# Gates of the last two branches ahead of the branches' own weights, in eight tiles; one attention over chosen keys among the heads

## The chip, the cores and the metric

The kernel runs on one core of a Trainium2 chip. Its engines are TensorE (PE; matmuls, and PEld for its weight loads), VectorE (DVE), ScalarE (ACT), GpSimd (POOL) and SyncE (SP), which issues the weight transfers. The metric is the device time of one execution in microseconds (us), the median of several runs. A difference is told in us or per cent of that time.

## The reference, cut to what matters

Two transformer blocks run one after the other over 256 tokens of width 1024. The first (a convolution, gated linear attention and a mixture of experts) is not touched. The second ends its mixing half with four branches, each gated by the block's normalised input u:

```python
u = rms_norm(h, norm_mix_pre[l])
z = u @ w_in[l]
(hq, hf, hi, hg, pz, sq, sk, sv, iq, ik, iw, mq) = jnp.split(z, split_pts, axis=-1)
y_a = hgrn2_mixer(hq, hf, hi, hg, lb_all[l], hgrn_norm[l])   # branch 0: a recurrence of 4 heads
y_b = pool_mixer(pz, pool_w[l], pool_scale[l])               # branch 1: means over windows
y_c = dsa_mixer(sq, sk, sv, iq, ik, iw)                      # branch 2: attention over chosen keys
...
y_m = mem_attention(mq, mk, mv)                              # branch 3: attention into a memory
for bi, y in enumerate((y_a, y_b, y_c, y_m)):
    term = jax.nn.sigmoid(u @ w_gate[l, bi]) * (y @ w_branch[l, bi])
    merged = term if merged is None else merged + term
h = h + rms_norm(merged @ w_out[l], norm_mix_post[l])
u = rms_norm(h, norm_ffn_pre[l])
gt, up = jnp.split(u @ w_ffn_gate_up[l], 2, axis=-1)
h = h + rms_norm((jax.nn.silu(gt) * up) @ w_ffn_down[l], norm_ffn_post[l])
```

A gate is a product of 256 × 1024 by 1024 × 1024; a branch's own product is 256 × 256 by 256 × 1024. All is in float32.

## The kernel before, in words

Each float32 operand of a large product is split into a rounded half and a remainder (hi and lo for weights, uh and ul or yh and yl for activations). A product is then three matmuls, in `Split.mm`: hi by hi (L186), hi by the activation's remainder (L187), the weights' remainder by hi (L188). The rounding of a weight piece of 128 × 2048 is one ScalarE instruction (L170); its remainder is split between VectorE (1280 columns, L172) and GpSimd (768 columns, L173). Pieces of 1 MB come by SyncE in a fixed order (`stream2`), and three buffers each for the incoming piece, for hi and for lo go round in turn. So the rounding of a piece waits until the piece three before it has been used by its last matmul.

In `second()` the order of calls is: `recall` (memory attention), `pooled`, `choose` for the two blocks of 128 tokens, `recur(0)` to `recur(3)` (the HGRN2 heads), `chosen(1)` and `chosen(0)` (attention over the chosen keys), then `branch(1)`, `branch(3)`, `branch(0)`, `branch(2)`, then w_out. A scheduler orders the instructions of each engine with this order as priority and with its own estimate of durations; it interleaves gate matmuls, which need only u, with the heads. Each engine then goes through its own list in order. From w_out on, the lists of ScalarE, VectorE and GpSimd are written out by hand (`tc.manual_schedule`), those of TensorE are not.

The last head, `recur(3)`, ends in a chain: decay products on TensorE (L1322) that VectorE copies under a mask (L1323), products with the values and the state (L1328, L1339, L1343), the square on ScalarE (L1349), the sum over the head (L1351), the root and its reciprocal (L1353, L1354), two multiplications (L1355, L1356) and the split into yh and yl (L178, L179). `chosen` has scores (L1444, L1451), a maximum (L1453), the exponential (L1382), sum and scaling (L1383, L1384), transposes (L1386) and the products with the values (L1398).

A branch of before computes, for each quarter of the 1024 columns (two blocks of 128), the gate's product in `dn.turned`, the branch's product with yh and yl, the sigmoid on ScalarE into one of two `sg` tiles, the product of both on VectorE (L1497), and the addition to `merged` on GpSimd (L1498). Its weights are taken ahead of its gate's two times two pieces. w_out takes `merged` split into four quarters mh and ml; `unit(t, half, kh)` is one product of 12 matmuls with 512 columns each. The normalisation and the split into uh and ul that the FFN needs follow.

Of the kernel before, what the change touches and what calls it, by code (L numbers as in the profile page):

```python
# [8 lines left out]
F32 = mybir.dt.float32  # L9
# [3 lines left out]
AF = mybir.ActivationFunctionType  # L13
OP = mybir.AluOpType
# [3 lines left out]
P = 128  # L18
T = 256
# [109 lines left out]
class Stream:  # L129
# [20 lines left out]
    def take(self):  # L150
        self.ahead(1)
        return self.ready.pop(0)
# [954 lines left out]
def second(tc, A, k, out):  # L1107
    nc = tc.nc
    V, S, G = nc.vector, nc.scalar, nc.gpsimd
    ident = k.cav("ident")  # L1110
    col2 = k.col2
    ones = k.cav("ones")
    k.n_a1, k.n_a2, k.n_sg = 6, 2, 2
    st_ = k.stream
    take = st_.take

    def pt(shape=(P, 512)):
        return k.ps.tile(list(shape), F32, tag="ps", name="pst", bufs=k.n_ps)

    def mx(shape=(P, 512)):  # L1120
        return k.ps.tile(list(shape), F32, tag="mx", name="mxt", bufs=8 - k.n_ps)

    with ExitStack() as es:
        ap = es.enter_context(tc.tile_pool(name="act2", bufs=1, side="right", reuse_waits="tile"))
        tp = es.enter_context(tc.tile_pool(name="tmp2", bufs=2, side="right", reuse_waits="tile"))
# [23 lines left out]
        sp = Split(nc, k.hi, k.lo)  # L1149
        dn = Dense(k, sp, take, pt)  # L1150
# [86 lines left out]
        for t in range(2):  # L1237
            p = mx((P, 4, P))
# [34 lines left out]
        yh, yl = {}, {}  # L1273
# [199 lines left out]

        merged = None

        def branch(b):

            nonlocal merged
            first = merged is None
            if first:  # L1480
                merged = ap.tile([P, NB, T], F32, tag="merged", name="merged")
            bh, bl = sp.weights(take(), 2)
            for half in range(2):
                def gate_in(i, o):
                    if i % 2 == 0:
                        return
                    blk = half * 4 + i - 1
                    p = pt((P, 2, T))
                    for j in range(2):
                        s = slice((blk + j) * P, (blk + j + 1) * P)  # L1490
                        sp.mm(p[:, j], lambda c: (bh[:, c, s], bl[:, c, s]), lambda c: (yh[b][:, c], yl[b][:, c]), 2)
                    sg = tp.tile([P, 2, T], F32, name="sg", bufs=k.n_sg)
                    S.activation(sg[:], dn.banks[i // 2][:], AF.Sigmoid)
                    if first:
                        V.tensor_tensor(merged[:, blk:blk + 2], sg[:], p[:], op=OP.mult)
                    else:
                        V.tensor_tensor(sg[:], sg[:], p[:], op=OP.mult)  # L1497
                        G.tensor_tensor(merged[:, blk:blk + 2], merged[:, blk:blk + 2], sg[:], op=OP.add)  # L1498

                dn.turned(X, gate_in)  # L1500

        recall(0)
        pooled()
# [2 lines left out]
        choose(0)  # L1506
        recur(0)
        recur(1)
        recur(2)
        recur(3)  # L1510
        chosen(1)
        chosen(0)
        branch(1)
        branch(3)
        post = ap.tile([P, 2, D], F32, tag="ln2", name="post")
        nc.sync.dma_start(post[:], A["rows2"][:, 2 * D:4 * D].rearrange("o (a d) -> o a d", a=2)
                            .to_broadcast([P, 2, D]))
        branch(0)
        branch(2)
        gain = ap.tile([P, D], F32, tag="gain", name="gain")  # L1520
        nc.sync.dma_start(gain[:], A["rows2"][:, 5 * D:].to_broadcast([P, D]))

# [19 lines left out]
        for q in range(4):  # L1542
            s = slice(2 * q, 2 * q + 2)
# [13 lines left out]
        with tc.manual_schedule(engines={E.Activation, E.DVE, E.Pool}):  # L1557
# [7 lines left out]
            a, b = [add_normed(t, banks[t], post[:, 0]) for t in range(2)]  # L1565
# [74 lines left out]
        a, b = [add_normed(t, banks[t], post[:, 1], True) for t in range(2)]  # L1640
        with tc.manual_schedule(engines={E.Activation, E.DVE, E.Pool}):
            go(a, a, a, b, a, b, b, b)
        for t in range(2):
            for half in range(2):
                s = slice(half * 512, half * 512 + 512)
# [3 lines left out]
def body(tc, A, out):  # L1649
# [6 lines left out]
    with ExitStack() as es:  # L1656
# [25 lines left out]
        with ExitStack() as mid:  # L1682
# [15 lines left out]
            experts(tc, A, k)  # L1698
        k.stream.open([A["s2"][i] for i in range(A["s2"].shape[0])])
        second(tc, A, k, out)  # L1700


# [31 lines left out]
def stream2(f):  # L1734

    w, gate, br = f["w_in_2"][0], f["w_gate_2"][0], f["w_branch_2"][0]
    gu, dn = f["w_ffn_gate_up_2"][0], f["w_ffn_down_2"][0]
    out = []

    def add(m):  # L1740
        out.extend(m.reshape(2, 4, P, 512).transpose(0, 2, 1, 3).reshape(2, P, PIECE))

    def rows(m):

        out.append(m.reshape(2, P, D).transpose(1, 0, 2).reshape(P, PIECE))

    add(np.concatenate([w[:, 1536:1792], w[:, 1024:1280]], axis=1))
    add(w[:, 512:1024])
    add(np.concatenate([w[:, 2760:3016], w[:, 2688:2752], w[:, 2048:2112], w[:, 2752:2760], w[:, 2112:2176],
                        np.zeros((D, 56), np.float32)], axis=1))  # L1750
    add(w[:, 2176:2688])
    add(w[:, 0:512])
    add(np.concatenate([w[:, 1792:2048], w[:, 1280:1536]], axis=1))
    for b in (1, 3, 0, 2):
        rows(br[b])
        for half in range(2):
            add(gate[b][:, half * 512:half * 512 + 512])
    for half in range(2):
        add(f["w_out_2"][0][:, half * 512:half * 512 + 512])
    for i in range(11):  # L1760
        add(np.concatenate([gu[:, 256 * i:256 * i + 256], gu[:, D_FF + 256 * i:D_FF + 256 * i + 256]], axis=1))
        if i:
            rows(dn[256 * i - 256:256 * i])
    rows(dn[2560:])
    m = f["w_mem_kv_2"][0].reshape(2, 4, P, 512).transpose(0, 2, 1, 3).reshape(2, P, PIECE)
    return np.stack(out), m
# [66 lines left out]
```

## Time and profile before

| | us |
|---|---|
| median of 3 runs (1702.92 to 1703.82) | 1702.96 |
| profiled execution, its own time | 1702.62 |
| its span | 1700.8 |
| TensorE busy in the span | 1491.7 (88%) |
| VectorE, ScalarE, GpSimd busy | 547.6, 468.5, 483.3 |

The granted clock of TensorE is 0.957 of full over the whole span. The span has three parts: the first block's dense half to about 310 us, its experts, bound by the transfer of their weights, to about 1190 us, and the second block. The change is in the second block, between 1240 and 1510 us. A line of the timeline gives start, duration, engine, source line, operation, what is written and read, tile and count, and in brackets the idle time of the engine ahead of it with the instruction that ended it.

### The profile page before, as it was taken

What the parts mean: (1) busy time and instruction counts of PE and PEld (TensorE: products, weight loads), DVE (VectorE), ACT (ScalarE), POOL (GpSimd) and SP (SyncE); (2) the same over time, 40 slices, a digit from 0 to 9 for tenths busy, and PEclk for the clock granted to TensorE, in tenths of its full rate; (3) what the DMA queues carried; (4) which work ended last, traced back from release to release, by engine and by line L of the source; (5) the groups of instructions that cost most, each with busy time, mean ns of one, the idle gap of its engine ahead of it and who ended that gap; (6) DMA issues with size and microseconds to landing.
All of it is one profiled execution on the core that took longest, in us unless ns stands there. A gap on an engine that the chain in (4) does not pass through costs nothing.

```text
span 1700.8 us, 23674 instructions
## 1 busy us (share of the span) xinstructions
PE 1491.7 (88%) x9903; PEld 993.1 (58%) x9903; DVE 547.6 (32%) x1037; ACT 468.5 (28%) x640; POOL 483.3 (28%) x331
## 2 busy tenths in 40 slices
PE   8999999984899878887877878787799998999998
PEld 6999996332353323232332323232499997979997
DVE  5888686100111000010000000000463856453233
ACT  6435652100301000010000000000465544563433
POOL 6777832000000000000000000000354554556563
PEclk9999999996999989899998999999999998999999
DMA  7453689999999999999999999999744332534552
GB/s 279 153 179 142 232 309 359 425 426 426 426 426 426 426 427 426 427 426 427 426 426 427 426 426 427 426 427 426 308 174 149 124 124 100 186 145 178 185 187 75
DMA packets 75838, 533.21 MB, mean 314 GB/s; under 512 B 8641, under 2 KB 9153, under 8 KB 12114
## 3 DMA queue, kind: packets, MB, share of 16 engines
q1 hardware_dynamic: 74178, 526.61, 76.2%
q10 hardware_dynamic: 1552, 5.07, 0.8%
q8 instruction: 79, 1.29, 0.3%
q14 instruction: 29, 0.24, 0.0%
HBM read 530.60 MB, written 1.05 MB: 313 GB/s over the span
## 4 chain that ended last, share of the span: by engine, by line
DMA 39%; PE 31%; DVE 3%; ACT 2%; issue 1%; DVEq 0%; ACTq 0%; SPq 0%
DMA w<-in_w_dram 39%; PE pst L188 6%; PE pst L187 6%; PE pst L186 6%; PE pst L890 2%; PE mxt L187 2%; PE mxt L186 2%; PE pst L912 2%; PE mxt L188 2%; PE pst L879 1%; PE acc L961 1%; ACT hi L170 1%; DVE lo L172 0%; PE mxt L1322 0%; PE pst L1175 0%
## 5 line engine op out<-in xcount | busy, mean ns | idle before, releaser
L173 POOL TENSOR_TENSOR lo<-w,hi 128x768 fp32r<-128x768 f32 (+2 forms) x112 | 380.6, 3404 | 352.9 <-ACT hi L170 323.8
L890 PE MATMUL pst<-w,xe 128*32 128x512 f32 x2048 | 342.7, 662 | 85.4 <-DMA w<-in_w_dram 83.6
L890 PEld LDWEIGHTS pst<-w,xe 128*32 128x32 f32 x2048 | 81.3, 119 | 323.3 <-issue 164.8
L170 ACT ACTIVATE hi<-w 128x2048 fp32r<-128x2048 f32 (+1 forms) x112 | 209.0, 1868 | 211.5 <-PE pst L187 117.9
L938 POOL TENSOR_TENSOR sw<-S,Wt 128x64 f32<-128x64 f32 x128 | 33.4, 292 | 816.9 <-DVE S L687 564.4
L187 PE MATMUL pst<-ul,hi 128*128 128x256 f32 x736 | 208.8, 284 | 0.0
L188 PE MATMUL pst<-uh,lo 128*128 128x256 f32 x736 | 207.9, 283 | 0.3 <-DVE lo L172 0.3
L186 PE MATMUL pst<-uh,hi 128*128 128x256 f32 x736 | 208.1, 283 | 0.0
L905 DVE TENSOR_TENSOR hd<-si,pst 128x128 f32<-128x128 f32 x64 | 18.4, 287 | 557.7 <-ACT si L904 557.7
L912 PE MATMUL pst<-w,hd 128*32 128x512 f32 x1024 | 168.3, 607 | 26.1 <-DVE hd L905 23.8
L172 DVE TENSOR_TENSOR lo<-w,hi 128x1280 fp32r<-128x1280 f32 (+1 forms) x77 | 122.6, 1592 | 152.4 <-ACT hi L170 142.5
L879 PEld LDWEIGHTS pst<-S,x 128*128 128x128 f32 x1024 | 123.5, 196 | 64.0 <-issue 63.1
L893 ACT ACTIVATE hs<-pst 128x512 f32<-128x512 f32 x32 | 19.1, 597 | 452.0 <-PE pst L890 452.0
L188 PEld LDWEIGHTS pst<-uh,lo 128*128 128x128 f32 x736 | 138.4, 188 | 2.3 <-DVE lo L172 0.9
L186 PEld LDWEIGHTS pst<-uh,hi 128*128 128x128 f32 x736 | 138.8, 189 | 1.5 <-ACT il L1266 0.3
L187 PEld LDWEIGHTS pst<-ul,hi 128*128 128x128 f32 x736 | 138.4, 188 | 1.7 <-issue 0.5
L879 PE MATMUL pst<-S,x 128*128 128x64 f32 x1024 | 133.4, 283 | 3.5 <-issue 2.5
L423 DVE SCALAR_TENSOR_TENSOR mxt<-U,cols,mxt 128x256 f32<-128x256 f32 x232 | 113.2, 488 | 7.0
L186 PE MATMUL pst<-xh,hi 128*128 128x256 f32 x352 | 98.6, 283 | 6.4 <-ACT hi L170 6.4
L188 PE MATMUL pst<-xh,lo 128*128 128x256 f32 x352 | 98.1, 285 | 0.6 <-DVE lo L172 0.6
L187 PE MATMUL pst<-xl,hi 128*128 128x256 f32 x352 | 98.5, 283 | 0.0
L961 PE MATMUL acc<-ys,WT 64*128 64x512 f32 x256 | 82.9, 615 | 16.6 <-DVE ys L920 16.6
(411 smaller groups left out, 1921.0 us busy)
## 6 DMA issues: line engine op xcount, KB each, us to landing
w<-in_w_dram SPq DMA_DIRECT2D x384, 1024.0 KB, 19.5
w<-in_s_dram SPq DMA_DIRECT2D x108, 1024.0 KB, 4.8
w<-in_wm_dram SPq DMA_DIRECT2D x2, 1024.0 KB, 20.4
rows<-in_rows_dram ACTq DMA_DIRECT2D x1, 1572.0 KB
w<-in_s_dram SPq DMA_DIRECT2D x4, 256.0 KB, 6.6
xn<-in_x_by_dram ACTq DMA_DIRECT2D x1, 1024.0 KB
mem<-in_mem_dram ACTq DMA_DIRECT2D x1, 1024.0 KB, 11.4
w<-in_rows_dram SPq DMA_DIRECT2D x1, 1024.0 KB, 19.5
```

Source lines behind the costliest of these rows:

```text
L170: nc.scalar.activation(hi[:, s], raw[:, s], AF.Copy)
L172: nc.vector.tensor_tensor(lo[:, v], raw[:, v], hf[:, v], op=OP.subtract)
L173: nc.gpsimd.tensor_tensor(lo[:, g], raw[:, g], hf[:, g], op=OP.subtract)
L186: mm(out, lh, rh, start=start and c == 0, stop=False, skip_group_check=True)
L187: mm(out, lh, rl, start=False, stop=False, skip_group_check=True)
L188: mm(out, ll, rh, start=False, stop=stop and c == n - 1, skip_group_check=True)
L423: V.scalar_tensor_tensor(cv[:, blk] if j == 30 else acc, U[:, blk, j:j + T], cols[:, cw + j:cw + j + 1], acc, op0=OP.mult, op1=OP.add)
L879: nc.tensor.matmul(pg[:, c], x1[:, t, c * P:(c + 1) * P], Sx[:, t], start=t == 0, stop=t == 1)
L890: nc.tensor.matmul(ph[g:g + 32, :], xe[:, c, e * CAP:(e + 1) * CAP], w[:, c % 4, :], start=c == 0, stop=c == NB - 1)
L912: nc.tensor.matmul(py[g:g + 32, :], hd[:, j, e], w[:, j % 2, half * 512:half * 512 + 512], start=j == 0, stop=j == 3)
L938: G.tensor_tensor(sw[:, t, dup, :m].rearrange("p (e s) -> p e s", e=n), Sx[:, t].rearrange("p (e s) -> p e s", e=n), wts[t], op=OP.mult)
L961: nc.tensor.matmul(acc[t][half][:], wt_, y, start=False, stop=pr == 31, skip_group_check=True)
```

## The change

The sg tiles are eight instead of two. A new function `gates(b)` computes all four quarters of a gate, with their sigmoids; `branch` is given them and only computes the branch's product, the multiplication and the addition. For branches 1 and 3 gate and branch follow each other. For branches 0 and 2 both gates are computed first, then both branches. Branch 2 adds on VectorE, the others on GpSimd as before. `chosen(1)` stands between `recur(1)` and `recur(2)`. The order of the weight pieces follows: of branches 1 and 3 the gate's pieces, then the branch's; then the gates' pieces of 0 and 2, then the weights of branch 0 and of branch 2.

```diff
--- before.py
+++ after.py
@@ -1110,7 +1110,7 @@
     ident = k.cav("ident")
     col2 = k.col2
     ones = k.cav("ones")
-    k.n_a1, k.n_a2, k.n_sg = 6, 2, 2
+    k.n_a1, k.n_a2, k.n_sg = 6, 2, 8
     st_ = k.stream
     take = st_.take
 
@@ -1473,31 +1473,38 @@
 
         merged = None
 
-        def branch(b):
+        def gates(b):
+
+            sgs = []
+            for half in range(2):
+                def gate_in(i, o):
+                    if i % 2:
+                        sg = tp.tile([P, 2, T], F32, name="sg", bufs=k.n_sg)
+                        S.activation(sg[:], dn.banks[i // 2][:], AF.Sigmoid)
+                        sgs.append(sg)
+
+                dn.turned(X, gate_in)
+            return sgs
+
+        def branch(b, sgs, add=G):
 
             nonlocal merged
             first = merged is None
             if first:
                 merged = ap.tile([P, NB, T], F32, tag="merged", name="merged")
             bh, bl = sp.weights(take(), 2)
-            for half in range(2):
-                def gate_in(i, o):
-                    if i % 2 == 0:
-                        return
-                    blk = half * 4 + i - 1
-                    p = pt((P, 2, T))
-                    for j in range(2):
-                        s = slice((blk + j) * P, (blk + j + 1) * P)
-                        sp.mm(p[:, j], lambda c: (bh[:, c, s], bl[:, c, s]), lambda c: (yh[b][:, c], yl[b][:, c]), 2)
-                    sg = tp.tile([P, 2, T], F32, name="sg", bufs=k.n_sg)
-                    S.activation(sg[:], dn.banks[i // 2][:], AF.Sigmoid)
-                    if first:
-                        V.tensor_tensor(merged[:, blk:blk + 2], sg[:], p[:], op=OP.mult)
-                    else:
-                        V.tensor_tensor(sg[:], sg[:], p[:], op=OP.mult)
-                        G.tensor_tensor(merged[:, blk:blk + 2], merged[:, blk:blk + 2], sg[:], op=OP.add)
-
-                dn.turned(X, gate_in)
+            for q, sg in enumerate(sgs):
+                blk = 2 * q
+                p = pt((P, 2, T))
+                for j in range(2):
+                    s = slice((blk + j) * P, (blk + j + 1) * P)
+                    sp.mm(p[:, j], lambda c: (bh[:, c, s], bl[:, c, s]), lambda c: (yh[b][:, c], yl[b][:, c]), 2)
+                m = merged[:, blk:blk + 2]
+                if first:
+                    V.tensor_tensor(m, sg[:], p[:], op=OP.mult)
+                else:
+                    V.tensor_tensor(sg[:], sg[:], p[:], op=OP.mult)
+                    add.tensor_tensor(m, m, sg[:], op=OP.add)
 
         recall(0)
         pooled()
@@ -1506,17 +1513,19 @@
         choose(0)
         recur(0)
         recur(1)
+        chosen(1)
         recur(2)
         recur(3)
-        chosen(1)
         chosen(0)
-        branch(1)
-        branch(3)
+        branch(1, gates(1))
+        branch(3, gates(3))
         post = ap.tile([P, 2, D], F32, tag="ln2", name="post")
         nc.sync.dma_start(post[:], A["rows2"][:, 2 * D:4 * D].rearrange("o (a d) -> o a d", a=2)
                             .to_broadcast([P, 2, D]))
-        branch(0)
-        branch(2)
+
+        sg0, sg2 = gates(0), gates(2)
+        branch(0, sg0)
+        branch(2, sg2, V)
         gain = ap.tile([P, D], F32, tag="gain", name="gain")
         nc.sync.dma_start(gain[:], A["rows2"][:, 5 * D:].to_broadcast([P, D]))
 
@@ -1751,10 +1760,12 @@
     add(w[:, 2176:2688])
     add(w[:, 0:512])
     add(np.concatenate([w[:, 1792:2048], w[:, 1280:1536]], axis=1))
-    for b in (1, 3, 0, 2):
-        rows(br[b])
-        for half in range(2):
-            add(gate[b][:, half * 512:half * 512 + 512])
+    for some in ((1,), (3,), (0, 2)):
+        for b in some:
+            for half in range(2):
+                add(gate[b][:, half * 512:half * 512 + 512])
+        for b in some:
+            rows(br[b])
     for half in range(2):
         add(f["w_out_2"][0][:, half * 512:half * 512 + 512])
     for i in range(11):
```

On TensorE, at the end of the last head. Of before (E are the masked decays, uh and ul the split u, mxt and pst banks of PSUM, yh_8078 and yl_8079 the split output of branch 0):

```order
L188 MATMUL pst<-uh,lo 128x256
L1322 MATMUL mxt<-E 128x128 x8
L1328 MATMUL mxt<-vp,kd 128x64
L1322 MATMUL mxt<-E 128x128 x2
L1328 MATMUL mxt<-vp,kd 128x64 x2
L1339 MATMUL mxt<-att,vp 64x128
L1343 MATMUL mxt<-E,st_8085 64x64
L1339 MATMUL mxt<-att,vp 64x128
L1343 MATMUL mxt<-E,st_8085 64x64 x2
L1351 MATMUL mxt<-sq,cb 128x256
L1444 MATMUL mxt<-skT,sqT 128x256 x4
L186 MATMUL pst<-yh_8078,hi 128x256 x2
```

And of the change, around its last gate matmul:

```order
L186 MATMUL pst<-uh,hi 128x256
L1322 MATMUL mxt<-E 128x128 x2
L187 MATMUL pst<-ul,hi 128x256
L1322 MATMUL mxt<-E 128x128 x2
L188 MATMUL pst<-uh,lo 128x256
L186 MATMUL pst<-yh_8078,hi 128x256
L187 MATMUL pst<-yl_8079,hi 128x256
L188 MATMUL pst<-yh_8078,lo 128x256
```

Before, the last head's tail and chosen(0)'s scores come in one piece and 192 gate matmuls follow it further on in the list; now the list's last gate matmul stands between the decay products L1322, followed by matmuls of branch 0, and what stands behind is the head's tail, chosen(0), the rest of branches 0 and 2, and w_out.

On VectorE, the same place. Of before (lo<-w,hi is the remainder of a weight piece):

```order
L1323 COPY_PREDICATED att<-cl,mxt 128x256 x3
L172 TENSOR_TENSOR lo<-w,hi 128x1280
L1323 COPY_PREDICATED att<-cl,mxt 128x256 x2
L1330 COPY st_8085<-mxt 128x64
L1323 COPY_PREDICATED att<-cl,mxt 128x256 x2
L1332 SCALAR_TENSOR_TENSOR st_8085<-st_8085,dl,mxt 128x64 x2
L1354 RECIPROCAL rs<-rs 128x256
L1355 SCALAR_TENSOR_TENSOR rs<-mxt,cols_85,rs 128x256
L1451 SCALAR_TENSOR_TENSOR lg<-mxt,neg_8272 128x256 x2
```

And of the change:

```order
L1323 COPY_PREDICATED att<-cl,mxt 128x256 x4
L1330 COPY st_8085<-mxt 128x64
L172 TENSOR_TENSOR lo<-w,hi 128x1280
L1323 COPY_PREDICATED att<-cl,mxt 128x256 x2
L1332 SCALAR_TENSOR_TENSOR st_8085<-st_8085,dl,mxt 128x64 x2
L1354 RECIPROCAL rs<-rs 128x256
L1451 SCALAR_TENSOR_TENSOR lg<-mxt,neg_8324 128x128 x4
L1355 SCALAR_TENSOR_TENSOR rs<-mxt,cols_85,rs 128x256
L1453 TENSOR_REDUCE nm<-lg 128x2 x2
```

A weight remainder stands ahead of the last two masked copies, and chosen(0)'s four score rows come between the reciprocal L1354 and the multiplication L1355 of the head's normalisation.

On ScalarE, behind w_out, where uh is made for the FFN. Of before:

```order
L1094 ACTIVATE rss<-rss,eps_rms 128x1
L170 ACTIVATE hi<-w 128x2048
L178 ACTIVATE uh<-pst 128x4x128
L170 ACTIVATE hi<-w 128x2048
L178 ACTIVATE uh<-pst 128x4x128
L170 ACTIVATE hi<-w 128x2048
L1163 ACTIVATE junk,rss<-mxt 128x512 x2
```

And of the change:

```order
L1093 ACTIVATE rss<-rss 128x1
L1094 ACTIVATE rss<-rss,eps_rms 128x1
L170 ACTIVATE hi<-w 128x2048 x3
L178 ACTIVATE uh<-pst 128x4x128 x2
L1163 ACTIVATE junk,rss<-mxt 128x512 x2
```

The three roundings and the two uh alternated; now the three roundings come first.

## Rows read from the trace of the kernel before

**Rows 1.** Table of windows: window, length, busy time (count) by engine, PEclk, DMA share, GB/s.

```profile
core 0: us, PE busy (x) PEld busy (x) DVE busy (x) ACT busy (x) POOL busy (x), PEclk, DMA share, GB/s
1418.00:1436.30 18.30, 13.12 (x60) 10.42 (x61) 12.93 (x30) 8.16 (x15) 4.15 (x2) 0.63 0.23 88
...
1240.00:1418.00 178.00, 177.50 (x1418) 167.85 (x1416) 112.47 (x219) 97.17 (x126) 90.80 (x60) 1.00 0.40 145
1436.30:1494.40 58.10, 58.10 (x403) 52.80 (x402) 29.06 (x44) 33.30 (x49) 35.45 (x16) 1.00 0.38 136
1496.00:1508.40 12.40, 8.31 (x28) 5.75 (x27) 8.24 (x11) 9.52 (x12) 7.63 (x2) 0.86 0.52 198
```

**Rows 2.** Timeline of TensorE around the end of the last head.

```profile
1411.04 0.28 PE L186 MATMUL pst<-uh,hi 128*128 128x256 f32 x1
...
1411.40 0.29 PE L186 MATMUL pst<-uh,hi 128*128 128x256 f32 x1
...
1423.23 0.69 PE L1339 MATMUL mxt<-att,vp 128*64 128x128 f32 x2
...
1431.07 0.80 PE L186 MATMUL pst<-yh,hi 128*128 128x256 f32 x2 [2.38 <-ACT yh L178]
...
1433.01 0.41 PE L187 MATMUL pst<-yl,hi 128*128 128x256 f32 x1
1433.22 0.41 PE L188 MATMUL pst<-yh,lo 128*128 128x256 f32 x1
```

**Rows 3.** Timelines of ScalarE and VectorE, 1417 to 1446.

```profile
1417.05 1.91 ACT L170 ACTIVATE hi<-w 128x2048 fp32r<-128x2048 f32 x1 [3.32 <-PE pst L187]
...
1425.43 1.28 ACT L1353 ACT_TABLE_LOAD   x1
...
1445.55 0.39 ACT L1382 ACTIVATE pe<-lg,nm 128x128 f32<-128x128 f32 x1
...
1418.99 1.49 DVE L172 TENSOR_TENSOR lo<-w,hi 128x1280 fp32r<-128x1280 f32 x1
1420.40 0.92 DVE L1323 COPY_PREDICATED att<-cl,mxt 128x256 f32<-128x256 int32 x2
...
1443.26 0.48 DVE L1451 SCALAR_TENSOR_TENSOR lg<-mxt,neg 128x128 f32<-128x128 f32 x2
```

**Rows 4.** Timelines of TensorE, VectorE and GpSimd during w_out.

```profile
1473.80 0.40 PE L188 MATMUL mxt<-hi,ml 128*128 128x512 f32 x1
...
1494.42 0.27 PE L1175 MATMUL pst<-dg,un 128*128 128x128 f32 x1
...
1470.63 0.69 DVE L179 TENSOR_TENSOR ml<-merged,mh 128x512 fp32r<-128x512 f32 x1 [2.05 <-ACT mh L178]
...
1478.98 1.67 DVE L179 TENSOR_TENSOR ml<-merged,mh 128x512 fp32r<-128x512 f32 x1 [1.85 <-ACT mh L178]
...
1478.24 1.86 POOL L173 TENSOR_TENSOR lo<-w,hi 128x768 fp32r<-128x768 f32 x1
```

**Rows 5.** Timelines of ScalarE, VectorE and GpSimd behind w_out.

```profile
1495.87 1.89 ACT L170 ACTIVATE hi<-w 128x2048 fp32r<-128x2048 f32 x1
1497.66 0.57 ACT L178 ACTIVATE uh<-pst 128x512 fp32r<-128x512 f32 x1
...
1500.14 3.71 DVE L172 TENSOR_TENSOR lo<-w,hi 128x1280 fp32r<-128x1280 f32 x1 [1.17 <-ACT hi L170]
...
1497.89 4.61 POOL L173 TENSOR_TENSOR lo<-w,hi 128x2048 fp32r<-128x2048 f32 x1 [4.09 <-ACT hi L170]
```

**Rows 6.** Timeline of TensorE, the first matmuls of the FFN.

```profile
1498.29 0.50 PE L186 MATMUL pst<-hi,uh 128*128 128x512 f32 x1 [1.93 <-ACT uh L178]
...
1504.50 0.79 PE L188 MATMUL pst<-hi,ul 128*128 128x512 f32 x1 [1.46 <-DVE ul L179]
1505.09 0.63 PE L186 MATMUL pst<-hi,uh 128*128 128x512 f32 x1
1505.52 0.63 PE L187 MATMUL pst<-lo,uh 128*128 128x512 f32 x1
...
1508.42 0.27 PE L1175 MATMUL pst<-dg,un 128*128 128x128 f32 x1
```

## The prediction

> **What bounds the kernel now.** I read the table of windows first. In the last 178 us before 1418.0 TensorE is busy 177.50 at full clock, and from 1436.3 to 1494.4 it is busy 58.10 of 58.10 [rows 1]. Here the bound is TensorE, and whatever VectorE, ScalarE or GpSimd save there is worth nothing. Two stretches between differ. From 1418.00 to 1436.30, where the last HGRN2 head ends, TensorE is busy 13.12 of 18.30 us at a mean granted clock of 0.63; work done is 13.12 × 0.63 = 8.3, so 10.0 us are lost. I call this dip 1. From 1496.0 to 1508.4, the normalisation between w_out and the FFN, it is busy 8.31 of 12.40 at 0.86, a loss of 5.3: dip 2. After it the FFN is full again, so a shift of dip 2's end reaches the end of the program one to one.
>
> Then I read TensorE's own timeline in dip 1. Its last decay products are waited for by the predicated copies (L1323); from the product at 1423.23 to the first branch product at 1431.07 only 7 us of small products run, with waits for the head's normalisation on ScalarE and VectorE between them. Matmuls of 256 columns start 0.12 us apart at 1411 (1411.04 to 1411.40 is three), and 0.21 apart at 1433 [rows 2]: the engine has fallen to the lower of its two clocks after standing still, and the stretch from 1436.3 is at full clock again [rows 1]. So an idle microsecond here costs up to two.
>
> **The change part by part.** Sums are made in the time of the profiled execution, 1702.62 (span 1700.8, 1.8 around it; the median of the runs is 0.34 higher).
>
> *Number of matmuls:* the same on both sides. What changes is which of them are left when the last head begins its tail. In the order of before, 192 gate matmuls stand behind the end of that head; at 0.12 us they are 23 us of work that the latencies of chosen(1) and chosen(0) hide under. In the order after, the last gate matmul stands among the decay products, and behind it come only 36 matmuls of branch 0 with yh, 48 of branch 2 with y, and w_out's 96. The gate work moves to where TensorE was busy 177.5 of 178, so it gains nothing there: 0, with bounds −0.5 (all idle of that stretch) and +2 (chosen(1)'s two rounds of softmax, now between the heads, make TensorE wait once).
>
> *Dip 1 after the change,* counted from the end of the last gate matmul:
> 1. The first w_out piece needs the buffer that this matmul frees: its rounding on ScalarE takes 1.91. VectorE's part of the remainder (L172, 1.49) follows, and in VectorE's order it stands ahead of the last two predicated copies (0.92) [rows 3]. L1339 follows at 4.3. Twelve matmuls of branch 0 that could lie beside this are 1.4 us of it.
> 2. From L1339 to the first product with the new yh before: 1431.07 − 1423.23 = 7.84 [rows 2]. Now four score rows (2 × 0.48) and two maxima of chosen(0) stand in VectorE's part of this chain, in place of two wider score rows, and four exponentials (4 × 0.39 = 1.56) stand ahead of the yh rounding on ScalarE [rows 3]. Part of that lies beside VectorE: I take +1.3, between 0.4 (all beside) and 2.5 (none). Sum 13.4.
> 3. The 36 matmuls: 16 at 0.21 and 20 at 0.12 are 5.8, the eight transposes and value products of chosen(0) 1.4 (an estimate: half of the 0.35 that one L1339 product shows at the lower clock). Sum 20.6. Then 48 × 0.12 = 5.7: 26.3.
> 4. w_out waits for the merged quarters. The adds are on VectorE now, with two inputs each. Beside a GpSimd remainder such instructions last longer in this trace: the ml subtraction takes 1.67 instead of 0.69 while the GpSimd remainder at 1478.24 runs 1.86 [rows 4]. I put 1.2 on the add, 1.2 on the ml behind it (nearer to the 1.67 row than to 0.69 plus a start), and 0.8 for the third mh, which is a ScalarE instruction of 0.57 (as uh [rows 5]) behind a rounding. Sum 29.5.
> 5. w_out: 96 × 0.234 (88 matmuls from 1473.80 to 1494.42 [rows 4]) = 22.5. Sum 52.0.
>
> The work in it at full clock: 36 and 48 matmuls 10.0, w_out 22.5, the twelve of step 1 1.4, and the head's tail with chosen(0) about 4.8 (an estimate from the 13.12 busy us of dip 1, of which some 9 are this tail, two thirds of them at the lower clock, and chosen(0)'s scores are half as wide). That is 38.7; lost are 13.3, against 10.0. **Term 1: +3.3**; without the waits of step 4 and with the clock staying up +0.4; with step 2 at its upper end and the 48 matmuls partly at 0.21, +5.
>
> For step 4 the Trainium skill has a rule ("SBUF — State Buffer", section "Who interferes with whom"): a VectorE instruction with two SBUF inputs and a GpSimd one that reads SBUF exclude each other for whole instructions. The trace agrees (1.67 for 0.69). By the rule an add or an ml that comes at the wrong moment waits out a whole 1.86; without it step 4 would be the third mh alone, and the term 0.9 or so. By it the change, which moves branch 2's adds from GpSimd to VectorE, makes four more instructions that such a remainder can hold up.
>
> *Dip 2.* The text of this code is not changed, but ScalarE's order is: before, the roundings of the three wide FFN pieces alternate with the two uh (hi 1495.87, uh 1497.66, hi, uh, hi); after, all three hi come first. VectorE's remainder L172 stands ahead of both ul, where before it stood between them.
> - First uh: 1495.87 + 3 × 1.9 + 0.57 = 1502.1, against a first product at 1498.29 [rows 6].
> - The remainder L172 runs beside GpSimd's wide remainder (1497.89, 4.61 us) and ended 3.71 after its start before, at 1503.85 [rows 5]; with the same end as the one bound, and 1502.5 + 1.49 = 1504.0 from GpSimd's end as the other, it comes out at the same time. The first ul ends 0.5 to 0.7 later, 1504.6.
> - Before, fourteen of the 24 matmuls of this group were done by then and the rest ran from 1504.50 to 1508.42 [rows 6]. Now two are, since the third needs ul. 22 × 0.234 gives 1509.8 (+1.3); with the first sixteen 0.43 apart, as from 1505.09 to 1505.52, 1512.9 (+4.5).
>
> TensorE will have stood longer here than before, where the lower clock came in too, so I take the middle: **term 2: +3.0.**
>
> *Smaller edits.* The branch weights are rounded later by as many pieces as the gates come earlier; at full TensorE this is hidden by the gate matmuls themselves. The post rows' DMA is issued three pieces later on SyncE and is read only in dip 2's normalisation, behind w_out. Two more table loads of ScalarE (1.28 each [rows 3]) lie in the stretch where ScalarE is busy 97 of 178 [rows 1]. GpSimd has four adds fewer and isn't the bound. All 0; were the cover of the table load gone, it is 1.3 once, inside term 1's upper bound.
>
> Sum: 0 + 3.3 + 3.0 = +6.3: 1708.9 for a profiled execution, 1709 for the median.
>
> **The rivals.**
> *No difference (about 1704.5).* The remainders of GpSimd fall beside other work than the adds, the clock does not fall further than now, and term 2 is at its lower end: 0.4 + 1.3 = +1.7. For it: before, w_out's quarters came through without a gap in 58.10 of 58.10, three of them next to GpSimd remainders. Against: then 23 us of gates stood ahead of them.
> *Faster (about 1698).* The sg tiles are ready, so merging has no ScalarE step between a branch product and its add, and the head's chain starts under the gate work: if the w_out rounding finds its buffer free before the decay copies (a piece that was ahead by one in the ring), step 1 falls to nothing, the twelve matmuls of branch 0 fill into step 2, and what stays idle is under 6 us, too little for a long stretch at the lower clock. Loss 4 to 5 instead of 10, term 2 +1.3: −4.5. It decides if the last gate matmul ends later than the last predicated copy. Against it: the copies stand behind L172 in VectorE's order, and L172 behind the rounding, which waits for that matmul.
> *Worse (about 1714).* chosen(1) between recur(1) and recur(2) is one in-order engine row more: its transposes wait for softmax (reciprocal and scaling of four heads) and everything behind waits too. TensorE has gates to fill, but a wait stops the row. Two stops of 1 us, and terms 1 and 2 at their upper ends: 2 + 5 + 4.4 = +11.4.
>
> **How the numbers follow.** Forecast 0.50; no difference 0.27; faster 0.11; worse 0.12. A measurement of this kernel tells about 0.2% (3.4 us) from no change. Faster by more: 0.11. Within: the second case less its upper tail and a little of the first, 0.28. Slower: 0.61. Range: the bounds of the terms give +0.7 to +11.4 (1703.4 to 1714), and reaching some way to the faster case 1701 to 1714. The likeliest case's own range is 1706 to 1712.5.
>
> **What would show it.** Step 1: a rounding on ScalarE that waits for the last gate product, then L172, then two predicated copies with TensorE idle. Step 2: some 13 us from the last gate matmul to the first yh product. Step 4: a gap in TensorE ahead of w_out's first products, with a VectorE add or ml over 1.5 us. Dip 2: three wide roundings in a row, the first FFN product near 8 us after w_out's last one (3.9 now). The prediction is wrong if dip 1 loses under 10 us, which the table of windows tells at once, or if the stretch before it is no longer full.

## The result and the profile after

The changed kernel takes 1713.62 us (median of 4 runs, 1712.79 to 1713.85), the kernel before 1702.94 us in the same comparison: a ratio of 1.0065, 95% interval 1.0053 to 1.0077. It is slower by 0.65%, where 1709 was forecast and 1701 to 1714 given; 1.0065 times 1702.96 is 1714.03, just beyond the upper end. The profiled execution took 1712.79 us, its span is 1710.7, 9.9 longer than before.

The table of windows of the changed kernel, cut where one kind of work ends and the next begins (window, length, busy time and count by engine, granted clock of TensorE, DMA share, GB/s):

```profile
1300.00:1340.00 40.00, 38.19 (x296) 34.21 (x296) 30.34 (x72) 24.49 (x37) 15.56 (x13) 1.00 0.31 106
1340.00:1446.70 106.70, 106.68 (x848) 101.15 (x848) 67.58 (x129) 56.46 (x62) 53.00 (x41) 1.00 0.39 142
1446.70:1474.80 28.10, 20.50 (x140) 17.73 (x138) 19.11 (x36) 11.01 (x20) 8.71 (x6) 0.82 0.18 65
1474.80:1498.90 24.10, 23.14 (x96) 17.84 (x96) 11.90 (x16) 10.78 (x15) 9.60 (x3) 1.00 0.42 153
1498.90:1518.30 19.40, 12.05 (x41) 9.48 (x41) 12.16 (x17) 13.23 (x24) 7.54 (x2) 0.74 0.42 160
```

And of the kernel before, from the end of w_out to the second group of transposes, cut as the last row above:

```profile
1494.42:1508.42 14.00, 9.91 (x42) 7.33 (x41) 8.98 (x12) 10.86 (x16) 7.63 (x2) 0.88 0.53 194
```

Against [rows 1]: TensorE is full until 1446.7 but for 1.8 us, two waits at 1334 and 1338; the dip of the last head loses 28.1 − 20.50 × 0.82 = 11.3 us where it lost 10.0, and now has w_out directly behind it; and the stretch behind w_out is 19.4 us long, of which 12.05 × 0.74 = 8.9 is work, so 10.5 are lost there where it was 5.3 in 14.0 us. From here the rest has the same length in both: the second group of transposes begins at 1508.42 before and 1518.32 after, 192.4 us from the end of either span.

TensorE's timeline, first at the two waits and at the first scores of chosen(1), then at the places that [rows 2], [rows 4] and [rows 6] show of before:

```profile
1334.09 0.68 PE L1322 MATMUL mxt<-E 128*128 128x128 f32 x4 [0.59 <-POOL att L1312]
...
1338.38 0.68 PE L1322 MATMUL mxt<-E 128*128 128x128 f32 x4 [1.23 <-DVE kd L1310]
...
1388.69 1.14 PE L1444 MATMUL mxt<-skT,sqT 64*128 64x256 f32 x8
...
1446.48 0.37 PE L188 MATMUL pst<-uh,lo 128*128 128x256 f32 x1
...
1451.93 0.43 PE L1328 MATMUL mxt<-vp,kd 64*128 64x64 f32 x2 [2.11 <-DVE att L1323]
1452.41 0.43 PE L1339 MATMUL mxt<-att,vp 128*64 128x128 f32 x2
...
1460.05 0.78 PE L1386 MATMUL mxt<-ca,pe 128*128 128x128 f32 x2 [3.88 <-DVE sm L1383]
1460.90 0.58 PE L186 MATMUL pst<-yh,hi 128*128 128x256 f32 x1
...
1474.83 0.51 PE L186 MATMUL mxt<-hi,mh 128*128 128x512 f32 x1 [1.06 <-ACT mh L178]
...
1498.65 0.39 PE L188 MATMUL mxt<-hi,ml 128*128 128x512 f32 x1
1501.54 3.52 PE L1175 MATMUL pst<-dg,un 128*128 128x128 f32 x16 [2.50 <-DVE dg L1169]
1508.61 0.79 PE L186 MATMUL pst<-hi,uh 128*128 128x512 f32 x1 [3.55 <-ACT uh L178]
1509.20 0.63 PE L187 MATMUL pst<-lo,uh 128*128 128x512 f32 x1
...
1518.32 0.27 PE L1175 MATMUL pst<-dg,un 128*128 128x128 f32 x1
```

The engines that it waits for, of the changed kernel (ScalarE, VectorE and GpSimd):

```profile
1446.37 1.92 ACT L170 ACTIVATE hi<-w 128x2048 fp32r<-128x2048 f32 x1 [2.66 <-PE pst L187]
...
1496.50 0.60 ACT L1539 ACTIVATE junk<-mxt 128x512 f32<-128x512 f32 x1 [3.65 <-PE mxt L188]
...
1502.59 5.49 ACT L170 ACTIVATE hi<-w 128x2048 fp32r<-128x2048 f32 x3
...
1448.45 3.08 DVE L172 TENSOR_TENSOR lo<-w,hi 128x1280 fp32r<-128x1280 f32 x1
...
1470.33 3.18 DVE L172 TENSOR_TENSOR lo<-w,hi 128x1280 fp32r<-128x1280 f32 x1
...
1506.37 4.11 DVE L172 TENSOR_TENSOR lo<-w,hi 128x1280 fp32r<-128x1280 f32 x1 [3.49 <-ACT hi L170]
...
1448.36 1.82 POOL L173 TENSOR_TENSOR lo<-w,hi 128x768 fp32r<-128x768 f32 x1 [3.94 <-ACT hi L170]
```

The reader sees the chain of the tail: the rounding that waits for the gate matmuls, the remainder on VectorE that lasts 3.08 us instead of 1.49 beside GpSimd's (1448.36), and TensorE's 2.11 us of waiting for the two copies behind it. In the kernel before two such remainders overlapped at this place as well, but VectorE's began first, at 1418.99 [rows 3], 0.05 us ahead of GpSimd's, and it was GpSimd's that became longer:

```profile
1419.04 3.11 POOL L173 TENSOR_TENSOR lo<-w,hi 128x768 fp32r<-128x768 f32 x1 [2.31 <-ACT hi L170]
```

Now GpSimd's begins 0.09 us ahead, and VectorE's is the longer one, with TensorE behind it. Behind w_out a second thing stands out. The square of tile 0's second half (junk, L1539) begins at 1496.50, 2.4 us before w_out's end at 1498.89. In the kernel before the same instruction began 5.7 us before it:

```profile
1488.76 0.60 ACT L1530 ACTIVATE junk<-mxt 128x512 f32<-128x512 f32 x1 [1.15 <-PE mxt L188]
```

So tile 0's normalisation, some 5 us long, lay beside w_out then and sticks out now: TensorE stands for 2.50 us, and the 16 transposes behind take 3.52 instead of 1.95, at a granted clock of 0.53 where the w_out matmuls had 1.00:

```profile
1501.54:1505.06 3.52, 3.52 (x16) 3.22 (x16) 1.34 (x3) 3.46 (x6) 0.45 (x1) 0.53 0.07 28
```

The reason is TensorE's list, in which the scheduler orders w_out's 96 matmuls, presumably by when it expects the merged quarters. Its last 25 were all of tile 1 before; now tile 0's second bank gets its last product 11 matmuls before the end.

The 9.9 us are thus 4.5 up to w_out's end (1498.89 − 1494.42) and 5.4 behind it. Of the 4.5, 1.3 fall among the heads (1.8 lost against 0.5), which leaves 3.2 from the last gate matmul to w_out's end. The windows show about 2.2 of these as lost time (11.3 and, in w_out, 1.0, against 10.0); where the other 1.0 lies they don't show.

### The profile page after: what moved, and what is told of

It is laid out like the page before. It is cut to its first block, busy times and chain, and to the rows that moved or that the text cites. A ratio compares the mean times of both kernels' runs of the same rounds, so it can differ in the third digit from the quotient of the medians.

```text
span 1710.7 us, 23677 instructions
## 1 busy us (share of the span) xinstructions
PE 1492.4 (87%) x9903; PEld 990.9 (58%) x9903; DVE 557.2 (33%) x1041; ACT 471.2 (28%) x642; POOL 472.4 (28%) x327
## 4 chain that ended last, share of the span: by engine, by line
DMA 38%; PE 32%; DVE 3%; ACT 2%; issue 1%; SPq 0%; DVEq 0%; ACTq 0%
DMA w<-in_w_dram 38%; PE pst L186 6%; PE pst L188 6%; PE pst L187 6%; PE pst L890 2%; PE pst L912 2%; PE mxt L187 1%; PE mxt L188 1%; PE mxt L186 1%; PE pst L879 1%; DVE lo L172 1%; PE acc L961 1%; PE mxt L1322 1%; PE pst L1175 0%; ACT hi L170 0%
## 5 line engine op out<-in xcount | busy, mean ns | idle before, releaser
L173 POOL TENSOR_TENSOR lo<-w,hi 128x768 fp32r<-128x768 f32 (+2 forms) x112 | 374.7, 3351 | 370.1 <-ACT hi L170 350.9
L172 DVE TENSOR_TENSOR lo<-w,hi 128x1280 fp32r<-128x1280 f32 (+1 forms) x77 | 126.9, 1648 | 149.3 <-ACT hi L170 147.6
## 6 DMA issues: line engine op xcount, KB each, us to landing
mem<-in_mem_dram ACTq DMA_DIRECT2D x1, 1024.0 KB, 11.3
```

The lines of the kernel that those rows point to most:

```text
L172: nc.vector.tensor_tensor(lo[:, v], raw[:, v], hf[:, v], op=OP.subtract)
L173: nc.gpsimd.tensor_tensor(lo[:, g], raw[:, g], hf[:, g], op=OP.subtract)
```

## The experiments

The theory with which they began: the three places add up, with the move of chosen(1) behind the first, the used-up gates behind the second, and w_out's order behind the third. Rival 1: the additions on VectorE, which the remainders hold up, make the time. Rival 2: the move of chosen(1) makes it. All ratios are to the kernel before, with 95% intervals; the kernel before was timed again beside each group of them, with medians of 1702.1 to 1703.2.

**Either half of the change alone, and one gate at a time.** First the change without its move of chosen(1):

```diff
         recur(1)
-        chosen(1)
         recur(2)
         recur(3)
+        chosen(1)
         chosen(0)
```

> The change without its move of chosen(1), which stays behind the last head. Theory: the time added by the change has three places, the stretch of the heads (+1.3 us, chosen(1) between them), the tail of the last head (+3.2, no gate matmuls left to lie beside it) and the normalisation behind w_out (+5.4, because TensorE's list ends tile 0's second half only 11 matmuls before w_out's end, before 25). In this kernel the list has 25 again and ScalarE's roundings alternate with uh, so the third part should be under 1; the first is gone; the tail has chosen(1)'s and chosen(0)'s latencies and no gates behind them: +3 to +6. About 1707 to 1709. Rival 1 (the adds on VectorE and the shared port make the time): as the change, 1713. Rival 2 (the move of chosen(1) makes it): 1703.

Measured 1714.45 us (1.0068, 1.0054 to 1.0082). Then the kernel before with that move alone (the same lines the other way round):

> The kernel before with only chosen(1) moved between recur(1) and recur(2). Theory: the stretch of the heads loses 1.3 as in the change, the tail keeps its 192 gate matmuls, w_out's order is that of before: +1 to +2, about 1704.5. Rival 1 (adds on VectorE): 1703, nothing changed there. Rival 2 (the move of chosen(1) makes the change's time): 1711 to 1713.

Measured 1712.09 us (1.0060, 1.0047 to 1.0074). Then the gates one by one:

```diff
-        sg0, sg2 = gates(0), gates(2)
-        branch(0, sg0)
-        branch(2, sg2, V)
+        branch(0, gates(0))
+        branch(2, gates(2), V)
...
-    for some in ((1,), (3,), (0, 2)):
+    for some in ((1,), (3,), (0,), (2,)):
```

> The change, but gates(0), branch(0), gates(2), branch(2) one after the other, with the weight pieces in that order. TensorE's list then has all 192 matmuls of gate 2 behind the last head, after branch 0's. Theory: the tail is as before or better for chosen(0), and the part behind w_out as in the change (11 matmuls before its end, three roundings in a row, +5.4): 1708 to 1710. If the gates that are left do not matter: 1713. Rival 1 (adds on VectorE): 1713.

Measured 1722.59 us (1.0115, 1.0100 to 1.0131). All three expectations failed, and with them the sum of separate parts. Windows of the gates-only kernel and of the chosen-only kernel, at the waits of the heads and at the stretch that loses:

```profile
1300.00:1340.00 40.00, 38.20 (x298) 34.41 (x295) 30.75 (x72) 24.50 (x37) 15.18 (x12) 1.00 0.30 106
1450.00:1477.00 27.00, 14.05 (x86) 11.88 (x85) 16.10 (x39) 12.42 (x27) 9.88 (x6) 0.66 0.22 75
```

```profile
1300.00:1340.00 40.00, 40.00 (x317) 36.59 (x314) 31.84 (x96) 23.43 (x36) 12.18 (x11) 1.00 0.30 106
1410.00:1447.00 37.00, 25.27 (x128) 20.47 (x127) 21.94 (x53) 9.74 (x19) 7.99 (x13) 0.70 0.23 85
```

So the 1.8 us among the heads come with the gates and not with chosen(1): the gates-only kernel has both waits, the chosen-only kernel has neither. They lie in the first head; in the change chosen(1) begins only at 1388.69 (its first scores, L1444), in a stretch that is full.

At the stretch that loses, the first loses 27 − 14.05 × 0.66 = 17.7 us: no gates are left, and both attentions over chosen keys come behind the last head, with one wait of 6.25 us for a scaled exponential:

```profile
1473.27 0.45 PE L1386 MATMUL mxt<-ca,pe 128*128 128x128 f32 x1 [6.25 <-DVE pe L1384]
```

The second loses 37 − 25.27 × 0.70 = 19.3, while 192 gate matmuls stand behind it in the list: between recur(2)'s decay products and branch 0's products the list has none, and those that stood there before now stand earlier, beside chosen(1). Behind w_out neither loses more than the kernel before (first FFN product 3.88 us after the transposes began, as at 1494.42 and 1498.29). So w_out ends 11.8 and 9.8 us later with either half alone, and 4.5 with both. By the lists, the gates that are pulled ahead cover the last head, which the chosen-only kernel leaves bare, and the earlier chosen(1) no longer stands behind the last gate, as it does in the gates-only kernel. The move of chosen(1) by itself costs as much as the change (rival 2's number), but not as a part of it.

The third kernel, with the gates one by one, does both things that cost: like the chosen-only kernel it has no gate matmul from 1415.5 to 1456.4 and loses 41 − 31.77 × 0.67 = 19.7 us there, and like the change it has TensorE waiting behind w_out (2.40 us ahead of the transposes, three roundings ahead of uh).

```profile
1415.00:1456.00 41.00, 31.77 (x163) 26.07 (x162) 20.98 (x53) 12.43 (x22) 10.38 (x13) 0.67 0.20 75
```

**The additions on GpSimd again:** `branch(2, sg2, G)` for `branch(2, sg2, V)`.

> The change with branch 2's four additions on GpSimd again. Theory: they move on GpSimd from 0.7 to 1.3 each and lose the waits beside the remainders, w_out begins within 1 us of where it did, and tile 0 still ends late (13 matmuls before w_out's end instead of 11): 1712 to 1714. Rival 1 (adds on VectorE against the shared port make the time of the change): 1705 or less.

Measured 1714.16 us (1.0070, 1.0057 to 1.0084). Rival 1 falls: the time is that of the change within the intervals. That w_out would begin within 1 us failed: it begins 2.25 us later (1477.08), and its first product waits 2.46 us for mh instead of 1.06. So VectorE was the better place for w_out's start, but no difference in the whole time is shown.

**TensorE's order in w_out.** First the code's own order, by adding TensorE to the engines ordered by hand:

```diff
-        with tc.manual_schedule(engines={E.Activation, E.DVE, E.Pool}):
+        with tc.manual_schedule(engines={E.Activation, E.DVE, E.Pool, E.PE}):
```

> The change with TensorE's matmuls of w_out in the order in which the code calls them (the order written out by hand now holds for TensorE too). Tile 0 is then ready 36 matmuls (8.4 us) before w_out's end instead of 11. Theory: the 2.5 us of standing still behind w_out and the half clock of the 16 transposes go, and the first FFN matmul comes about 4 us after w_out's last: dip 2's extra 5.4 falls to 1 to 2, the rest stays: 1709 to 1710. Rivals 1 and 2: 1713, since neither adds nor chosen(1) are touched.

Measured 1719.50 us (1.0100, 1.0085 to 1.0115), a miss, which the timeline explains: the code has tile 0's transposes ahead of the last bank's 24 products, so TensorE stands 4.73 us ahead of them, and the first bank's order makes it wait for ml.

```profile
1481.72 0.79 PE L188 MATMUL mxt<-hi,ml 128*128 128x512 f32 x1 [3.46 <-DVE ml L179]
...
1503.08 0.55 PE L1175 MATMUL pst<-dg,un 128*128 128x128 f32 x1 [4.73 <-DVE dg L1169]
```

The second attempt orders by quarters and puts all products ahead of the transposes (with `unit` for a quarter q of the contraction):

```diff
+            w.append(sp.weights(take(), 4))
+            for q in range(2):
+                for t, half in ((0, 0), (1, 0), (0, 1)):
+                    unit(t, half, q)
+            for t, half in ((0, 0), (1, 0), (0, 1)):
+                unit(t, half, 2)
+                unit(t, half, 3)
+            for q in range(4):
+                unit(1, 1, q)
```

> The change with TensorE's list for w_out written by hand: quarters 0 and 1 for three of the four banks first, then both banks of tile 0, tile 1's second bank last. Tile 0's second half ends 24 matmuls (5.6 us) before w_out's end, with no bank waiting for a quarter longer than in the change. Theory (the late end of tile 0 makes the 5.4 us behind w_out): TensorE's 2.5 us ahead of the transposes go, the first FFN matmul comes 4 to 6 us after w_out's last (9.7 in the change): 1707 to 1710. If the 5.4 is instead ScalarE's three roundings ahead of uh: 1712 to 1713.

Measured 1708.69 us (1.0035, 1.0021 to 1.0049), 4.9 us under the change and within the expectation. TensorE behind w_out:

```profile
1500.63 0.40 PE L188 MATMUL mxt<-hi,ml 128*128 128x512 f32 x1
1500.87 1.95 PE L1175 MATMUL pst<-dg,un 128*128 128x128 f32 x16
1504.74 0.50 PE L186 MATMUL pst<-hi,uh 128*128 128x512 f32 x1 [1.93 <-ACT uh L178]
```

The 2.50 us and the slow transposes are gone, and the way from w_out's end to the first FFN product is 3.87 again. The second group of transposes begins 13.4 us after w_out's end, against 19.4 in the change; w_out itself ends 2.0 us later (1500.87 against 1498.89). With tile 0 early the first uh also came directly behind one rounding instead of three, so two causes behind w_out were removed together, and no run here separates them. In the rows of the change the way from w_out's end to the first FFN product is 5.8 us longer than before: 2.6 until the transposes begin, 1.6 for the slow transposes and 1.6 of longer waiting for uh. The matmuls behind it then give 0.4 back.

**Holding gates back for the tail.** The next kernels have that w_out order and edges of order on TensorE: a quarter (half, kh) of gate 2's matmuls goes behind a marked matmul of the last head, and products of branch 0 go behind gate 2. (Only the line that places the quarters is shown.)

```diff
-        sg0, sg2 = gates(0), gates(2)
+        sg0, sg2 = gates(0), gates(2, (((0, 0), ("sums", 0)), ((0, 1), "turn"), ((1, 0), "decay"), ((1, 1), "sum")))
```

> As the kernel with the hand-written w_out list, and gate 2's 192 matmuls are held for the last head: by edges of order on TensorE they come behind the decay sums, the transposes, the decay products and the sum of recur(3), and branch 0's second half comes behind the last of them. Nothing else is changed. Theory (the tail costs time because no gate matmuls are left to lie beside it): the waits of the tail (2.1, 3.9) fall under 2 together and the clock stays up, 5 to 9 us less than with the hand-written w_out list alone, so 1699 to 1704, at or under the kernel before. If the tail's time is not the missing cover but the remainders of the branch pieces on VectorE: within 2 us of that kernel.

Measured 1712.59 us (1.0062, 1.0049 to 1.0076), 3.9 us over the kernel without held gates, where 5 to 9 less were expected. Its windows, three rows:

```profile
1410.00:1430.00 20.00, 16.12 (x102) 14.34 (x102) 12.48 (x21) 7.04 (x9) 8.12 (x11) 0.83 0.31 106
1430.00:1460.00 30.00, 29.73 (x238) 27.75 (x236) 15.62 (x28) 14.42 (x18) 10.12 (x7) 1.00 0.34 131
1459.20:1480.00 20.80, 15.37 (x106) 13.34 (x104) 14.93 (x24) 10.00 (x17) 11.23 (x6) 0.92 0.28 93
```

The last head is now full (29.73 of 30 at full clock), as the theory says. But the third head, before it, loses 20 − 16.12 × 0.83 = 6.6, since its gates are the ones held, and behind the last gate (1459.1) the attention and the two branches lose 20.8 − 15.37 × 0.92 = 6.7. With 144 held instead of 192:

```diff
-(((0, 0), ("sums", 0)), ((0, 1), "turn"), ((1, 0), "decay"), ((1, 1), "sum"))
+(((0, 1), ("sums", 0)), ((1, 0), "turn"), ((1, 1), "sum"))
```

> As the kernel with 192 held gate matmuls, but only 144 are held for the last head, from the second quarter on (behind decay sums, transposes and the sum over the head); chosen(1) still among the heads. In the kernel with 192 held the idle time moved to the third head, whose tail had no gates left (some 7 us lost from 1410 to 1430). Theory (one supply of gate matmuls covers one stretch or another): the third head gets 48 back (5.7 us), the last head has 48 fewer; the sum of idle time changes little, 1708 to 1712. If the place and not the sum decides, it is under 1705.

Measured 1712.67 us (1.0058, 1.0045 to 1.0072), 0.7 over the expected range: the cover moves and the sum stays, for both of them some 4 us over the kernel without held gates. Then chosen(1) behind the last head again, which takes its need for cover out of the heads, and the held gates beside the tail and both attentions:

```diff
-        chosen(1)
         recur(2)
         recur(3)
+        chosen(1)
         chosen(0)
...
+(((0, 0), "decay"), ((0, 1), "sum"), ((1, 0), ("score", 1)), ((1, 1), ("score", 0)))
```

> Gates ahead, with the hand-written w_out list, and chosen(1) behind the last head as in the kernel before. Gate 2's 192 matmuls are held for that head's tail and for chosen(1) and chosen(0) (behind the last decay product, the sum over the head, and the scores of either), and branch 0's products come behind the first 96 of them. So the heads have the same gate matmuls as in the kernel before, and the 7.8 us of the head's normalisation has 60 gate matmuls beside it instead of none. Theory: dip 1 falls from 10 us to 3 to 5 (the last head's first phase has no gates now): 1696 to 1702. Rival (chosen(1)'s and chosen(0)'s own latencies then come to the end of the list): 1703 or more.

> As the kernel with the tail covered, but the first 48 of the held gate matmuls are let go behind the first decay sums of the last head instead of its last decay product, so its first phase has cover and the tail 48 less. Theory: within 3 us of that kernel, and better by what the first phase loses there (2 to 4 us): 1694 to 1700. Rival: as there.

Measured 1707.59 us (1.0032, 1.0020 to 1.0044) and, with the first 48 let go behind ("sums", 0), 1706.56 us (1.0024, 1.0014 to 1.0034): 7 us under the change, but still slower than before, where both expectations had them faster; they lie in the rival's range (1703 or more). In the first, the stretch with the normalisation of the last head and both attentions, which the held gates now cover, is full, while the first phase of that head now loses 30 − 24.33 × 0.94 = 7.1:

```profile
1410.00:1440.00 30.00, 24.33 (x170) 21.11 (x170) 15.44 (x25) 11.34 (x13) 11.96 (x11) 0.94 0.29 106
1440.00:1472.00 32.00, 32.00 (x274) 30.98 (x274) 20.32 (x44) 21.35 (x35) 15.57 (x8) 1.00 0.38 132
```

In the second the windows are

```profile
1410.00:1440.00 30.00, 27.52 (x191) 24.41 (x190) 19.36 (x34) 12.39 (x15) 12.23 (x11) 0.89 0.37 141
1440.00:1472.00 32.00, 30.88 (x258) 29.03 (x257) 19.58 (x36) 19.79 (x33) 16.59 (x8) 1.00 0.29 100
1472.00:1498.30 26.30, 24.50 (x96) 19.17 (x97) 15.14 (x22) 13.53 (x23) 11.08 (x4) 0.94 0.41 150
```

The last head's dip is 30 − 27.52 × 0.89 = 5.5 where it was 10.0 before. But w_out now loses 26.3 − 24.50 × 0.94 = 3.3 at its start, where the kernel before lost nothing, and 1.8 us stay among the first heads. Last, 24 gate matmuls between branch 2's second and third quarter (and, in a second kernel, another 24 moved within the last head):

```diff
-((1, 1), ("score", 0)))
+((1, 1, 0), ("score", 0)), ((1, 1, 1), "last")))
```

> As the kernel with the tail covered and the first phase of the last head covered too (e14), but the last 24 gate matmuls (2.9 us) come between the second and the third quarter of branch 2's products instead of ahead of branch 0. In e14, as in the change, all 48 products of branch 2 stand in one piece ahead of w_out, and w_out's first 8 us lose 3.9 to waits for merged, mh and ml; in the kernel before the gates stood between those products and w_out started without a wait. Theory: 2 to 3.9 of it come back: 1702.5 to 1704.5. If the waits are the remainders that hold the adds, and not the missing work between: within 1 us of e14's 1706.6.

> As e15, and of the 48 gate matmuls in the last head's first phase 24 wait until the last decay products. Theory: cover moves between two waits of one chain, the sum changes by less than 1.5 us either way against e15.

Measured 1708.28 (1.0033, 1.0021 to 1.0045) and 1708.84 us (1.0036, 1.0021 to 1.0050). The expectation for the second held (0.6 us between the two); that for the first failed: w_out begins without a wait, but the gate piece holds its buffer longer, and the rounding of w_out's own piece comes late in its turn:

```profile
1479.04 0.55 PE L188 MATMUL mxt<-lo,mh 128*128 128x512 f32 x1 [4.09 <-DVE lo L172]
```

Two waits ahead of and in w_out (1.23 and 1.45 us) were traded for one that is longer. No kernel tried here beats the one before. The best has 3.9 us more span up to the second group of transposes; its windows account for about 2 of them, and where the rest lies is open.

## Why the prediction was wrong, step by step

The direction and the mechanism of the first dip held; a size was wrong. The profiled executions differ by 9.9 us where the sum gave 6.3; of the 3.6 that are missing, 2.4 belong to term 2 and 1.3 to the heads.

- **Term 2, +3.0: this step failed.** Measured +5.4, above the upper end that the prediction gave it (4.5). Of its mechanism, three roundings ahead of the first uh and L172 ahead of both ul, all was there. But it began the count at the same distance from w_out's end as before (1495.87 is 1.45 after 1494.42). The roundings began 3.7 after it (1502.59), because tile 0 came late and ScalarE had tile 0's normalisation ahead of them. These 2.25 us are most of what the term lacked. The prediction treated w_out as 96 matmuls at 0.234, did not look at which bank they fill, and so put the late tile at nothing. 25 matmuls stand behind tile 0's last product before, 11 after. With w_out ordered by hand, tile 0's late end and the three roundings went together, and the median fell by 4.9 us.
- **Heads, 0 with bounds −0.5 and +2.** Measured +1.3, inside the bounds but not in the sum: two waits, 0.59 and 1.23 us, of decay products in the first head. The prediction allowed for waits by chosen(1); it was the gates that brought these, as the gates-only and the chosen-only kernel show. VectorE, on whose copy one of them waits, spends 3.00 us there on an L172 beside GpSimd's remainder (3.01 in the gates-only kernel); whether this makes the waits is not shown.
- **Term 1, +3.3.** From the last gate matmul's end (1446.85) to w_out's (1498.89) are 52.0 us, as summed, and the term measured +3.2. That it agrees so well is partly luck, as the steps fit less well than their sum. Step 1 took 5.6 instead of 4.3, since the remainder L172 ran against GpSimd's for 3.08 us (the sum had only put this effect into step 4). Step 2, from L1339 to the first yh product, took 8.5 instead of 9.1. Step 3 came out at 12.9, as summed, the waits of step 4 at 2.0 for 3.2, and w_out without them at 23.1 for 22.5. The last gate matmul at 1446.5 does stand ahead of the rounding, the copies and TensorE's wait. That missing gates make this dip is shown from both sides: where held gates lie beside the last head (192 held) or beside its normalisation and the attentions (the tail covered), the stretch is full, and the stretches that they were taken from lose instead.
- **Step 4's rule** (the Trainium skill, "SBUF — State Buffer", "Who interferes with whom"): the trace agrees, and in more places than the prediction used: 3.08, 3.18 and 4.11 us for the L172 of 1.49, each beside a GpSimd remainder that had begun before it.
- **The signs.** Dip 1 lost 11.3 us, so the sign of being wrong (under 10) did not come; the stretch before it was no longer quite full (1.8 us), which was the other one. The first yh product came 14 us after the last gate matmul, where "some 13" was given, and the first FFN product 9.7 us after w_out, where "near 8" was given.
- **The rivals.** "Worse" had the number, 1714, by luck: it added 2, 5 and 4.4 where 1.3, 3.2 and 5.4 came, and its stops of chosen(1) did not occur. "No difference" fell with both terms (3.2 and 5.4 for its 0.4 and 1.3). "Faster" fell because the last gate matmul ends (1446.85) before the last masked copies begin (1451.45); its argument that under 6 us of idle time are too little for the lower clock also goes against [rows 1], where 18.30 − 13.12 = 5.2 us of idle time stand beside a granted clock of 0.63.
- What the prediction did not see: the gates among the heads and the place of chosen(1) looked like separate edits. Either alone costs 9 to 12 us. Up to w_out's end the two together cost 4.5, less than either; the change then loses 5.4 behind w_out, which neither does alone.

## What to carry to other kernels

Work without dependences is one supply: before it is pulled ahead to fill small gaps, ask which long chain at the end then stands alone, and count the filler that is left there, in microseconds, against the chain. Where a scheduler orders matmuls, a change upstream can also reorder a product downstream; read which output is finished last, not only when the whole is. And test two edits that share such a supply together and apart, since their costs do not add.

## What was not expected of the hardware

Sixteen float32 transposes took 3.52 us at a granted clock of 0.53 after TensorE had stood for 2.50 us, and 1.95 without the wait, so this wait of 2.5 cost 4.1. The cost does not follow from the length of the wait alone: the same 16 took 3.35 us after 2.03 us of standing in the kernel with the additions on GpSimd, and 2.51 after 2.40 in the one with the gates one by one. In the window behind w_out the granted clock was 0.74 of full, before 0.88.
